# A gated MLP on one core: the opening of the first set reordered, one plain block fewer, and the second half of each block finished one step earlier

## The chip, the cores and the metric

The kernel runs on one core of a Trainium2 chip. The metric is device time in microseconds (us) of one execution, as the median over several runs. The core has five engines that run side by side and wait for one another through semaphores: TensorE (PE, matmuls into PSUM; PEld is its weight load), VectorE (DVE), ScalarE (ACT), GpSimd (POOL) and SyncE (SP, which issues DMAs). 16 DMA engines move data.

## The reference

x is 16 x 256 x 512 in f32 (4096 rows of 512), w1 is 512 x 4096, w2 is 2048 x 512.

```
h = x @ w1
gate, value = np.split(h, 2, axis=-1)
h = np.maximum(gate, 0) * value
return (h @ w2).astype(np.float32)
```

## The kernel before, in words

`fast_way` is the path that runs; `general_way` is a second one, taken only if sums of squares of the inputs (the `look` instructions on ScalarE, L190) come out of bounds. Everything is multiplied in f16 and summed in f32.

The 4096 rows are four **sets** of 1024, each set two halves of 512. The 2048 hidden columns are 16 **blocks** of 128; a block has a gate column and a value column of w1. Per set there are two stages. Stage 1 forms g = relu(gate) * value for 16 blocks. Stage 2 (`mm2_stream`, L279) multiplies g by w2 and writes the output.

Stage 1 uses a Strassen-Winograd scheme: seven products P1 to P7 (class `Block`, L195) in place of eight, each two matmuls of 512 columns. They need four sums of the x quarters (S1 to S4, `SUMS`, L185) and four sums of w1 quarters (T1 to T4, `TURNS`, L153) for each block. The products add up in three PSUM tiles: X, Y and W. P1 goes into X and ScalarE copies X into Y (L209). P5 goes into W, ScalarE scales it out as p5 (L216). P2 ends X. P6 adds to Y, ScalarE scales that out as u2 (L223). P3 ends W; VectorE forms c12 from W and u2 (L229) and then the first half of g from X and c12 (L230; called gX here). P7 adds to Y, VectorE forms c22 from Y and p5 (L235). P4 adds to Y; then `finish` forms the second half of g from Y and c22 (L241; called gY here).

The order is written out by hand. `SLOT` (L13) gives each product a place in a period of seven; P7 stands at 9 and P4 at 13, so they run in the period of the next block. A steady period on TensorE is P1, P5, P7 of the block before, P2, P6, P3, P4 of the block before, and in terms of one block j: P6(j), P3(j), P4(j-1), P1(j+1), P5(j+1), P7(j), P2(j+1), P6(j+1), P3(j+1), P4(j). The main loop (L540) emits `finish` of block j-1 only after P7 of block j (L552 to L554), so VectorE's order in a period is c12(j), gX(j), c22(j), gY(j-1). Every engine runs its instructions in the order in which they are emitted.

Stage 2 uses the same scheme with g in the place of x. It needs sums of g quarters (S1 to S4, L275, by GpSimd and for the last part by VectorE) and sums of w2 quarters (V). The w2 sums are made by DMA: SP copies parts of w2 (L532), GpSimd issues adding DMAs (`add_w2`, L163). Stage 2 of a set runs mostly behind stage 1 of that set, and its last 28 matmuls among the first blocks of the next set.

**The opening.** The first set can't use the scheme at once, since the w1 sums are not there yet. So its first `NPLAIN` = 4 blocks are plain: eight matmuls of 512 columns for each half of the rows (class `Plain`, L244). x comes as two loads of 512 KB through SP, and w1 columns 0 and 1 as two loads of 512 KB, in turn x, gates, x, values (L405 to L407). TensorE turns x by transposes (`turn_pair`, L371; `turn_half`, L379, for the second half of the rows, which GpSimd's queue loads as f16), VectorE and ScalarE copy the turned x to SBUF (L377, L384), and cast the w1 columns (`cast_w`, L390). The other w1 columns come in chunks (`CHUNKS`, L127) as casting DMAs on GpSimd's queue (`fetch_w1`, L350). Eight warm-up matmuls (`idle`, L171) run while nothing is there, and two more (`NFILL`) between the first turned x and the first gates. VectorE forms the x sums (`x_sum`, L449) beside the plain blocks of the second half.

GpSimd's own work in the first set, in its order (L523 to L539): w1 sums of blocks 4 to 11 two by two, with w2 loads between, then T1 and T2 of blocks 12 to 15, two adding DMAs, T3 and T4 of blocks 12 to 15, a third adding DMA, the load of x for set 2, then sums of g (L550). The w1 sums of blocks 0 to 3 are made by VectorE after the first set (L591).

Of the kernel before, what the change touches and what calls it, by code (L numbers as in the profile page):

```python
# [19 lines left out]
NWARM = 8  # L20
NFILL = 2
NPLAIN = 4
HIGH, LOW = 512.0, 32.0
# [76 lines left out]
def fast_way(ctx, tc, x2, w1, w2, out2, flag):  # L100
# [25 lines left out]

    CHUNKS = ((0, 2), (2, 2), (4, 2), (6, 2), (8, 4), (12, 4))  # L127
    place = {jb + i: (c, i) for c, (jb, n) in enumerate(CHUNKS) for i in range(n)}
# [66 lines left out]
    class Block:  # L195
# [41 lines left out]
        def P4(self):  # L237
            self.mm("P4", self.Y, False)

        def finish(self):  # L240
            nc.vector.scalar_tensor_tensor(out=self.g[:, self.jb, TH:], in0=self.Y, scalar=0.0,  # L241
                                           in1=self.c22, op0=MAX, op1=MULT)

    class Plain:  # L244
        def __init__(self, g, jb):
            self.g, self.jb = g, jb

        def open_x(self):
            self.X = psx.tile([P, TH], F32, name="X", tag="X")

        def open_w(self):
            self.W = psw.tile([P, TH], F32, name="W", tag="W")

        def mm(self, side, a, q, n=1):
            ts = slice(q * 256, (q + n) * 256)
            ps = self.W if side else self.X
            for e in range(4):
                name = (("B11", "B21"), ("B12", "B22"))[side][e // 2]
                nc.tensor.matmul(ps[:, ts], W(name, self.jb)[:, e % 2], a[:, e, ts], start=e == 0, stop=e == 3,  # L259
                                 skip_group_check=True)  # L260

        def close(self, h):
            v = tmp.tile([P, 2, TH], F32, name="v", tag="tmp")[:, 0]
            nc.scalar.activation(v, self.W, COPY, scale=GS)
            nc.vector.scalar_tensor_tensor(out=self.g[:, self.jb, h * TH:(h + 1) * TH], in0=self.X, scalar=0.0,
                                           in1=v, op0=MAX, op1=MULT)

# [11 lines left out]
    def mm2_stream(s, go):  # L279
# [14 lines left out]
        def step(name, b):  # L294
# [12 lines left out]
            elif name == "P2":  # L307
                yield from mm("P2", b, d["X"], False)
                d["o1"] = tmp.tile([P, DO], F32, name="o", tag="o", bufs=4)
                nc.scalar.activation(d["o1"][:, :HALF], d["X"], COPY, scale=1 / GS)  # L310
            elif name == "P6":
                yield from mm("P6", b, d["Y"], False)
                nc.scalar.activation(d["pu"][:, 1], d["Y"], COPY, scale=-1 / GS)
            elif name == "P3":
                yield from mm("P3", b, d["W"], False)
                nc.vector.scalar_tensor_tensor(out=d["o1"][:, HALF:], in0=d["W"], scalar=1 / GS, in1=d["pu"][:, 1],  # L316
                                               op0=MULT, op1=ADD)
                nc.sync.dma_start(out=out_v[s, 0, b], in_=d["o1"])
            elif name == "P7":
                yield from mm("P7", b, d["Y"], False)  # L320
                nc.vector.scalar_tensor_tensor(out=d["o2"][:, HALF:], in0=d["Y"], scalar=-1 / GS, in1=d["pu"][:, 0],
                                               op0=MULT, op1=ADD)
                if last and b == NB - 1:
                    nc.sync.dma_start(out=out_v[s, 1, b, :, HALF:], in_=d["o2"][:, HALF:])
            else:
                yield from mm("P4", b, d["Y"], False)
                nc.scalar.activation(d["o2"][:, :HALF], d["Y"], COPY, scale=1 / GS)
                if last and b == NB - 1:
                    nc.scalar.dma_start(out=out_v[s, 1, b, :, :HALF], in_=d["o2"][:, :HALF])
                else:  # L330
                    nc.sync.dma_start(out=out_v[s, 1, b], in_=d["o2"])
# [36 lines left out]
    xh = go["S2"][:, :NB]  # L368
    wl = g[:, NJ - 4:].rearrange("p a t -> p (a t)").bitcast(F32).rearrange("p (e g j) -> p e g j", e=4, g=2)

    def turn_pair(o, b0):  # L371
        for b in (b0, b0 + 1):
            ps = psw.tile([P, 4, P], F32, name="W", tag="W")
            for e in range(4):
# [4 lines left out]
    def turn_half(o, b0, copy):  # L379
        ps = psx.tile([P, 4, 2, P], F16, name="X", tag="X")  # L380
        for b in range(2):
# [7 lines left out]

    def cast_w(g_):  # L390
        nc.scalar.copy(out=wr[0][:, :2, g_], in_=wl[:, :2, g_])
        nc.vector.tensor_copy(out=wr[0][:, 2:, g_], in_=wl[:, 2:, g_])  # L392

# [10 lines left out]

    for i in range(2):  # L405
        nc.sync.dma_start(out=xf[:, 2 * i:2 * i + 2], in_=x_v[0, :, 2 * i:2 * i + 2])  # L406
        nc.sync.dma_start(out=wl[:, :, i], in_=w1_v[:, :, i, :2 * P])  # L407
    for t in ident.values():
        make_identity(nc, t)
    nc.gpsimd.tensor_copy(out=gate, in_=xf[:, 0, :1])  # L410
    fetch_w1(1, 0)
    fetch_w1(1, 1)
    for b in (0, 2):
        nc.gpsimd.dma_start(out=xh[:, b:b + 2], in_=x_v[0, :, NB + b:NB + b + 2])
# [4 lines left out]
    xo = x_tiles()  # L419
    plain = [Plain(g, jb) for jb in range(NPLAIN)]  # L420
    idle(NWARM)
    cast_w(0)
    turn_pair(xo, 0)
    idle(NFILL)
    plain[0].open_x()
    plain[1].open_x()
    for p in plain[:2]:
        p.mm(0, xo["A1"], 0)
    cast_w(1)
    turn_pair(xo, 2)  # L430
    for p in plain[:2]:
        p.open_w()
        p.mm(1, xo["A1"], 0)
    for p in plain[:2]:
        p.mm(0, xo["A1"], 1)
        p.mm(1, xo["A1"], 1)
        p.close(0)
    for p in plain[2:]:
        p.open_x()
        p.open_w()  # L440
        p.mm(0, xo["A1"], 0, 2)
        p.mm(1, xo["A1"], 0, 2)
        p.close(0)
        if p is plain[2]:
            turn_half(xo, 0, nc.vector.tensor_copy)
    turn_half(xo, 2, nc.scalar.copy)
    sums = list(SUMS)

# [3 lines left out]

    for p in plain:
        p.open_x()
        p.open_w()
        if p is plain[0]:
            for q in range(2):
                p.mm(0, xo["A2"], q)
                p.mm(1, xo["A2"], q)
        else:  # L460
            p.mm(0, xo["A2"], 0, 2)
            p.mm(1, xo["A2"], 0, 2)
        x_sum(xo)
        if p is not plain[-1]:
            p.close(1)
        look_x(0, p.jb)

    def look_w1(i):
        c, o = place[i // 2 * 2]
        look(wr[c][:, :, i % 2, o * P:(o + 2) * P], NX + i, 1024)  # L470

# [22 lines left out]
    for s in range(NS):  # L494
        for i in range(4 * NB):
            if s or i >= NPLAIN:
                LOOKS[s, i] = [lambda s=s, i=i: look_x(s, i)]
    LOOKS[0, NPLAIN].insert(0, lambda: plain[-1].close(1))

# [14 lines left out]
    for s in range(NS):  # L514
# [3 lines left out]
        blocks = {jb: Block(xo, g, jb) for jb in range(first, NJ)}  # L518
        plan = {jb * PERIOD + at: (jb, n) for jb in blocks for n, at in SLOT.items()}
        last = NJ * PERIOD  # L520
        stream = mm2_stream(s, go)
        if s == 0:
            w1_ops(nc.gpsimd, 4, 2)  # L523
            fetch_w2(0)
# [5 lines left out]
            w1_ops(nc.gpsimd, 10, 2)  # L530
            for to, v in ((V["T1"], V["B11"]), (v_12, w2_h[1]), (V["T4"], V["B21"])):
                nc.sync.dma_start(out=to, in_=v)  # L532
            for t in TURNS:
# [6 lines left out]
        for at in range(first * PERIOD, last + PERIOD):  # L540
            if at in plan:
                jb, n = plan[at]
                if n == "P1" and s and jb in (4, 8):
                    fetch_rows(s, 1 + jb // 4)
                if n == "P2" and s == 0 and jb in (11, 13, 15):
                    h = jb - 11
                    if h == 4:
                        add_w2("T4", "T2")
                    for m in ("S1", "S3")[:2 - h // 4]:
                        g_sum(nc.gpsimd, go, m, h, h + 2)  # L550
                getattr(blocks[jb], n)()
                ended = jb - (n == "P7") if n == "P7" or (n, jb) == ("P4", NJ - 1) else -1  # L552
                if ended in blocks:
                    blocks[ended].finish()  # L554
                if n == "P5":
                    for f in LOOKS.get((s, jb), ()):
                        f()
                if ended >= 0 and s:
                    if ended < NHC:
                        g_sum(nc.gpsimd, go, "S3", ended, ended + 1)  # L560
                        if s == 1 and ended in (1, 4):
                            cast_x(2 + ended // 4)
                    elif ended < NJ - BY_DVE:
                        for m in ("S1", "S2", "S4"):
                            g_sum(nc.gpsimd, go, m, ended - NHC, ended - NHC + 1)
            elif at >= last:
# [13 lines left out]
        if s + 1 < NS:  # L580
# [9 lines left out]
            if s == 0:  # L590
                w1_ops(nc.vector, 0, 2)  # L591
                w1_ops(nc.vector, 2, 2)
            advance(stream, MM2 - TAIL - 100 - done)
# [32 lines left out]
```

## Time and profile before

| | us |
|---|---|
| median of 3 runs | 312.03 (311.81 to 312.80) |
| the profiled execution | 312.03 |
| its span | 310.20 |
| TensorE busy | 301.7 |
| VectorE busy | 216.4 |
| ScalarE busy | 189.0 |
| GpSimd busy | 148.3 |
| granted TensorE clock | 1.00 |

The profile is one execution. Times in it run from the start of the span. A line of the order of time has the start, the duration, the engine, the line of the code (L followed by a number), the operation, the tiles that it writes and reads with their shapes, how many instructions are merged (x2), and in brackets the idle time of that engine just before and what ended it. SPq, POOLq and ACTq are DMA issues of an engine. Matmuls are pipelined: two of 512 columns are listed as 0.59 us, but the next two start 0.43 us after them.

### The profile page before, as it was taken

How to read it: one execution, taken by the hardware profiler on the slowest of the kernel's cores; microseconds unless marked ns; L12 is line 12 of the kernel's file. 1: busy time of each engine (PE TensorE's matmuls, PEld its weight loads, DVE VectorE, ACT ScalarE, POOL GpSimd, SP SyncE). 2: the span in 40 equal slices, each digit the busy share in tenths (PEclk: the TensorE clock that was granted, in tenths of full speed). 3: DMA queues.
4: the chain of work that ended last, by engine and by line, in shares of the span. 5: the costliest groups of instructions: out<-in, count | busy, mean ns of one | idle time of the engine just before them, and what ended most of it. 6: DMA issues, size and time to landing. Idle time of an engine off the chain costs nothing.

```text
span 310.2 us, 5097 instructions
## 1 busy us (share of the span) xinstructions
PE 301.7 (97%) x1867; PEld 183.0 (59%) x1867; DVE 216.4 (70%) x330; ACT 189.0 (61%) x450; POOL 148.3 (48%) x135
## 2 busy tenths in 40 slices
PE   8899999999999999999999999999999999999993
PEld 4654444588854444478874444458884444448883
DVE  1376888898548888884338888886526888888311
ACT  3347767647677667648847667656857667673230
POOL 5779997950003537992001435995000433898000
PEclk9999999999999999999999999999999999999999
DMA  7999979998315370045220110028311100000113
GB/s 246 200 202 204 215 195 231 203 120 231 121 73 101 71 169 0 3 92 158 90 104 35 34 34 2 0 52 151 139 71 68 34 6 30 0 2 0 69 68 139
DMA packets 33449, 30.74 MB, mean 99 GB/s; under 512 B 13872, under 2 KB 27952, under 8 KB 33200
## 3 DMA queue, kind: packets, MB, share of 16 engines
q0 software_dynamic: 10704, 11.54, 23.1%
q1 hardware_dynamic: 22576, 18.75, 20.5%
q8 instruction: 15, 0.25, 0.4%
q10 hardware_dynamic: 144, 0.13, 0.1%
q14 instruction: 10, 0.08, 0.1%
HBM read 24.12 MB, written 11.53 MB: 115 GB/s over the span
## 4 chain that ended last, share of the span: by engine, by line
PE 92%; DMA 2%; DVE 2%; issue 1%; ACT 1%; SPq 0%; DVEq 0%
PE Y L202 25%; PE X L202 17%; PE W L202 17%; PE Y L286 13%; PE W L286 8%; PE X L286 8%; DMA g<-in_w_dram 2%; PE W L259 2%; PE X L259 2%; DVE g_S L275 1%; ACT x_A L384 0%; SPq L406 0%; DVE wr L392 0%; DVE g L241 0%; DVE x_A L377 0%
## 5 line engine op out<-in xcount | busy, mean ns | idle before, releaser
L275 POOL TENSOR_TENSOR g_S<-g 128x512 f16<-128x512 f16 (+1 forms) x47 | 60.5, 1330 | 125.3 <-DVE g L241 123.4
L202 PEld LDWEIGHTS <-wt 128*128 128x128 f16 x480 | 46.9, 98 | 55.0 <-issue 0.2
L202 PE MATMUL X<-x_A,wr 128*128 128x512 f16 x240 | 71.4, 379 | 0.2 <-ACT Y L209 0.2
L202 PE MATMUL Y<-x_S,wt 128*128 128x512 f16 x240 | 71.4, 379 | 0.0
L202 PEld LDWEIGHTS <-wr 128*128 128x128 f16 x360 | 35.2, 98 | 41.1 <-issue 0.5
L229 DVE SCALAR_TENSOR_TENSOR cc<-W,pu 128x512 f32<-128x512 f32 x60 | 41.5, 692 | 23.8 <-ACT pu L223 23.7
L209 ACT COPY Y<-X 128x512 f32<-128x512 f32 x60 | 34.2, 570 | 37.7 <-PE X L202 37.1
L286 PEld LDWEIGHTS <-g_S 128*128 128x128 f16 x512 | 49.9, 98 | 6.4 <-DVE g_S L275 0.6
L235 DVE SCALAR_TENSOR_TENSOR cc<-Y,pu 128x512 f32<-128x512 f32 x60 | 41.5, 691 | 6.2 <-PE Y L202 0.2
L223 ACT ACTIVATE pu<-Y 128x512 f32<-128x512 f32 x60 | 35.8, 597 | 14.3 <-PE Y L202 14.3
L230 DVE SCALAR_TENSOR_TENSOR g<-X,cc 128x512 f16<-128x512 f32 x60 | 41.5, 691 | 2.3
L286 PEld LDWEIGHTS <-g 128*128 128x128 f16 x384 | 37.6, 98 | 8.2
L241 DVE SCALAR_TENSOR_TENSOR g<-Y,cc 128x512 f16<-128x512 f32 x60 | 40.8, 681 | 1.8 <-PE Y L202 1.8
L216 ACT ACTIVATE pu<-W 128x512 f32<-128x512 f32 x60 | 36.1, 602 | 0.0
L202 PE MATMUL W<-x_S,wr 128*128 128x512 f16 x120 | 35.7, 379 | 0.0
L202 PE MATMUL W<-x_S,wt 128*128 128x512 f16 x120 | 35.7, 379 | 0.0
L202 PE MATMUL Y<-x_A,wt 128*128 128x512 f16 x120 | 35.7, 379 | 0.0
L286 PE MATMUL X<-w,g 128*128 128x256 f16 x256 | 31.2, 272 | 0.0
L286 PE MATMUL Y<-v,g_S 128*128 128x256 f16 x256 | 30.6, 273 | 0.0
L316 DVE SCALAR_TENSOR_TENSOR o<-W,pv 128x256 f32<-128x256 f32 x16 | 6.8, 423 | 30.4 <-PE W L286 30.4
L275 POOL TENSOR_TENSOR g_S<-g,g_S 128x512 f16<-128x512 f16 x18 | 21.8, 1210 | 1.4
L275 POOL TENSOR_TENSOR g_S<-g_S,g 128x512 f16<-128x512 f16 x18 | 21.3, 1186 | 1.4
(69 smaller groups left out, 297.4 us busy)
## 6 DMA issues: line engine op xcount, KB each, us to landing
out_dram<-o SPq DMA_DIRECT2D x16, 256.0 KB, 2.2
out_dram<-pv SPq DMA_DIRECT2D x15, 256.0 KB, 2.0
x<-in_x_dram POOLq DMA_DIRECT2D x3, 1024.0 KB, 8.0
xn<-x SPq DMA_DIRECT2D x12, 256.0 KB, 3.2
wr<-in_w_dram POOLq DMA_DIRECT2D x4, 512.0 KB, 14.5
w<-in_w_dram POOLq DMA_DIRECT2D x4, 512.0 KB, 11.8
wr<-in_w_dram POOLq DMA_DIRECT2D x6, 256.0 KB, 8.8
g_S<-in_x_dram SPq DMA_DIRECT2D x2, 512.0 KB, 4.7
```

The lines of the kernel that those rows point to most:

```text
L202: nc.tensor.matmul(ps, W(wn, self.jb)[:, b], self.xo[xn][:, b, :], start=fresh and b == 0, stop=b == 1, skip_group_check=True)
L209: nc.scalar.copy(out=self.Y, in_=self.X)
L216: nc.scalar.activation(self.p5, self.W, COPY, scale=GS)
L223: nc.scalar.activation(self.u2, self.Y, COPY, scale=-GS)
L229: nc.vector.scalar_tensor_tensor(out=self.c12, in0=self.W, scalar=GS, in1=self.u2, op0=MULT, op1=ADD)
L230: nc.vector.scalar_tensor_tensor(out=self.g[:, self.jb, :TH], in0=self.X, scalar=0.0, in1=self.c12, op0=MAX, op1=MULT)
L235: nc.vector.scalar_tensor_tensor(out=self.c22, in0=self.Y, scalar=-GS, in1=self.p5, op0=MULT, op1=ADD)
L241: nc.vector.scalar_tensor_tensor(out=self.g[:, self.jb, TH:], in0=self.Y, scalar=0.0, in1=self.c22, op0=MAX, op1=MULT)
L259: nc.tensor.matmul(ps[:, ts], W(name, self.jb)[:, e % 2], a[:, e, ts], start=e == 0, stop=e == 3, skip_group_check=True)
L275: eng.tensor_tensor(go[n][:, h0:h1], go[i0][:, h0:h1], go[i1][:, h0:h1], op=op)
L286: nc.tensor.matmul(ps, go[gn][:, k, b * P:(b + 1) * P], V[vn][:, k, :], start=fresh and k == 0, stop=k == NHC - 1, skip_group_check=True)
L316: nc.vector.scalar_tensor_tensor(out=d["o1"][:, HALF:], in0=d["W"], scalar=1 / GS, in1=d["pu"][:, 1], op0=MULT, op1=ADD)
```

## The change

1. **Finishing.** `finish` is gone; its instruction (L241 before) is now the end of `P4`. So it is emitted ahead of c22 of the next block. Work of GpSimd that followed it (sums of g) is emitted after P4 too. In the first set the GpSimd sums S1 and S3 are emitted at P1 instead of P2.
2. **Opening.** Both x loads come first. Then come the gates of column 0, the gates of column 1, the values of both, and column 2 in two loads, all as f32 through SP and cast on ScalarE and VectorE. GpSimd's queue loads the second x half in two pieces, the second one only after the gates of column 1 have landed. Chunk 2 of w1 (casting DMA) now has columns 3 to 5.
3. **Plain blocks.** Three in place of four. The second half of the rows is worked in steps of a quarter set (256 columns), all three blocks of the first quarter, then all of the second. One warm-up matmul fewer between. Block 3 becomes a full `Block` (`lead`); its P1 stands between the gates and the values of the last plain step.
4. **Weight sums.** GpSimd makes the sums of block 3 ahead of those of blocks 4 and 5. VectorE makes those of blocks 0 to 2 later.
5. **w2.** The copies into v_12 are two of 512 KB instead of one of 1024 KB; copies are now T1, T3, T2, T4.
6. **Output.** In the last set the first half's output tile leaves in two DMAs.

```diff
-NFILL = 2
-NPLAIN = 4
+NFILL = 1
+NPLAIN = 3
...
-    CHUNKS = ((0, 2), (2, 2), (4, 2), (6, 2), (8, 4), (12, 4))
+    CHUNKS = ((0, 2), (2, 1), (3, 3), (6, 2), (8, 4), (12, 4))
...
         def P4(self):
             self.mm("P4", self.Y, False)
-
-        def finish(self):
             nc.vector.scalar_tensor_tensor(out=self.g[:, self.jb, TH:], in0=self.Y, scalar=0.0,
                                            in1=self.c22, op0=MAX, op1=MULT)
...
-                nc.sync.dma_start(out=out_v[s, 0, b], in_=d["o1"])
+                for n in (slice(0, HALF), slice(HALF, DO)) if last else (slice(0, DO),):
+                    nc.sync.dma_start(out=out_v[s, 0, b, :, n], in_=d["o1"][:, n])
...
-    for i in range(2):
-        nc.sync.dma_start(out=xf[:, 2 * i:2 * i + 2], in_=x_v[0, :, 2 * i:2 * i + 2])
-        nc.sync.dma_start(out=wl[:, :, i], in_=w1_v[:, :, i, :2 * P])
+    for b in (0, 2):
+        nc.sync.dma_start(out=xf[:, b:b + 2], in_=x_v[0, :, b:b + 2])
+    fetch_wl(0, 0)
+    fetch_wl(1, 0)
+    fetch_wl(0, 1, 2)
+    fetch_wl(2, 0)
+    fetch_wl(2, 1)
...
-    nc.gpsimd.tensor_copy(out=gate, in_=xf[:, 0, :1])
-    fetch_w1(1, 0)
-    fetch_w1(1, 1)
-    for b in (0, 2):
+    for b, land in ((0, xf[:, 0, :1]), (2, wl[0][:, 0, 0, P:P + 1])):
+        nc.gpsimd.tensor_copy(out=gate, in_=land)
         nc.gpsimd.dma_start(out=xh[:, b:b + 2], in_=x_v[0, :, NB + b:NB + b + 2])
...
+    whole = [Plain(g, jb, xo["A1"], 0, 0, 2) for jb in range(NPLAIN)]
+    parts = [[Plain(g, jb, xo["A2"], 1, q, 1) for jb in range(NPLAIN)] for q in range(2)]
+    lead = Block(xo, g, NPLAIN)
...
+    idle(NWARM)
+    turn_pair(xo, 0, psw, "W")
+    cast_w(0, 0)
+    idle(NFILL)
+    turn_pair(xo, 2, psx, "X")
+    whole[0].gates((0,))
+    cast_w(1, 0)
+    whole[0].gates((1,))
+    whole[1].gates()
+    cast_w(0, 1)
+    cast_w(1, 1)
+    whole[0].values()
+    whole[0].close()
+    cast_w(2, 0)
+    whole[1].values()
+    turn_half(xo, 0, nc.vector.tensor_copy)
+    whole[1].close()
+    cast_w(2, 1)
+    part(whole[2])
+    part(parts[0][0])
+    part(parts[0][1])
+    turn_half(xo, 2, nc.scalar.copy)
+    part(parts[0][2])
+    x_sum(xo)
+    for p in parts[1][:2]:
+        part(p)
+        x_sum(xo)
+        look_x(0, p.jb)
+    parts[1][2].gates()
+    lead.P1()
+    parts[1][2].values()
+    look_x(0, 2)
+    x_sum(xo)
...
         if s == 0:
+            w1_ops(nc.gpsimd, 3, 1)
             w1_ops(nc.gpsimd, 4, 2)
...
-            for to, v in ((V["T1"], V["B11"]), (v_12, w2_h[1]), (V["T4"], V["B21"])):
-                nc.sync.dma_start(out=to, in_=v)
+            for m, v in (("T1", "B11"), ("T3", "B12"), ("T2", "B22"), ("T4", "B21")):
+                nc.sync.dma_start(out=V[m], in_=V[v])
...
-                if n == "P2" and s == 0 and jb in (11, 13, 15):
+                if n == "P1" and s == 0 and jb in (11, 13, 15):
...
                 getattr(blocks[jb], n)()
-                ended = jb - (n == "P7") if n == "P7" or (n, jb) == ("P4", NJ - 1) else -1
-                if ended in blocks:
-                    blocks[ended].finish()
...
-                if ended >= 0 and s:
+                if n == "P4" and s:
...
-                w1_ops(nc.vector, 2, 2)
+                w1_ops(nc.vector, 2, 1)
```

## The prediction

> **What bounds the kernel now.** I read the page's busy table and its chain, then the order of time on the engines at the opening, inside one steady block, and at the end of the first set.
>
> ```profile
> PE 301.7 (97%) x1867; PEld 183.0 (59%) x1867; DVE 216.4 (70%) x330; ACT 189.0 (61%) x450; POOL 148.3 (48%) x135
> ...
> PE 92%; DMA 2%; DVE 2%; issue 1%; ACT 1%; SPq 0%; DVEq 0%
> ```
>
> TensorE is the bound. A change gains only where TensorE stands or where matmuls go; it loses wherever another engine comes late once in each block. TensorE's waits lie in the opening and at one place at 71 us:
>
> ```profile
> 10.68 1.03 PE L259 MATMUL W<-x_A,wr 128*128 128x256 f16 x8 [1.51 <-DVE x_A L377]
> ...
> 26.25 0.59 PE L202 MATMUL X<-x_A,wr 128*128 128x512 f16 x2 [0.23 <-ACT Y L209]
> ```
>
> After 31 us it stands once, 0.34 us at 71.37 for VectorE's S4. Now a steady block, TensorE, then ScalarE, then VectorE:
>
> ```profile
> 57.38 0.59 PE L202 MATMUL Y<-x_A,wt 128*128 128x512 f16 x2
> ...
> 59.53 0.59 PE L202 MATMUL Y<-x_S,wt 128*128 128x512 f16 x2
> ...
> 60.40 0.59 PE L202 MATMUL Y<-x_A,wt 128*128 128x512 f16 x2
> ```
> ```profile
> 57.15 0.60 ACT L223 ACTIVATE pu<-Y 128x512 f32<-128x512 f32 x1 [0.25 <-PE Y L202]
> ```
> ```profile
> 57.77 0.69 DVE L229 SCALAR_TENSOR_TENSOR cc<-W,pu 128x512 f32<-128x512 f32 x1 [0.20 <-ACT pu L223]
> 58.50 0.69 DVE L230 SCALAR_TENSOR_TENSOR g<-X,cc 128x512 f16<-128x512 f32 x1
> 59.30 0.69 DVE L235 SCALAR_TENSOR_TENSOR cc<-Y,pu 128x512 f32<-128x512 f32 x1
> 59.91 0.68 DVE L241 SCALAR_TENSOR_TENSOR g<-Y,cc 128x512 f16<-128x512 f32 x1
> ```
>
> P4 of the block before starts at 57.38, this block's at 60.40: 3.02 us for 14 matmuls, 0.216 each. VectorE's L235 (c22) reads Y after P7, and P4 adds into that same Y, so P4 may not start before c22 has ended. It ends at 59.99, 0.41 before P4. L241 finishes the block before, and no matmul waits for it at once. Last, GpSimd from 45 us, and VectorE behind it:
>
> ```profile
> 45.06 0.94 POOL L163 DMA_DIRECT2D v_T<-w  x1
> 48.36 0.88 POOL L163 DMA_DIRECT2D v<-w  x1 [2.36 <-DMA v<-w]
> 48.95 2.44 POOL L160 TENSOR_TENSOR wt<-wr 128x1024 f16<-128x1024 f16 x1
> 51.03 2.43 POOL L160 TENSOR_TENSOR wt<-wr,wt 128x1024 f16<-128x1024 f16 x1
> 53.10 1.19 POOL L163 DMA_DIRECT2D v<-v_T  x1
> 53.68 1.15 POOL L359 DMA_DIRECT2D x<-in_x_dram  x1
> 54.24 8.98 POOL L275 TENSOR_TENSOR g_S<-g 128x1024 f16<-128x1024 f16 x4
> 62.57 1.49 POOL L163 DMA_DIRECT2D v_T<-v  x1
> 63.20 3.02 POOL L275 TENSOR_TENSOR g_S<-g 128x1024 f16<-128x1024 f16 x1
> ```
> ```profile
> 64.80 1.97 DVE L275 TENSOR_TENSOR g_S<-g 128x1024 f16<-128x1024 f16 x1
> 66.70 2.35 DVE L275 TENSOR_TENSOR g_S<-g_S,g 128x2048 f16<-128x2048 f16 x2
> 68.97 2.35 DVE L275 TENSOR_TENSOR g_S<-g,g_S 128x2048 f16<-128x2048 f16 x2
> ```
>
> GpSimd works without a pause from 48.36 to 66.22. VectorE's second S2 (at 66.70 + half of 2.35 = 67.8) needs GpSimd's last S1, done at 66.22: 1.6 us to spare. From that S2 on, two S4 follow, and the second one's end at 71.32 releases TensorE at 71.37.
>
> **Part 1, the finishing step ahead of c22 (all blocks).** No instruction is added; L241 and L235 change places on VectorE. TensorE's order is P6, P3, P4 of the block before, P1, P5, P7, and so on, so the new VectorE order is c12, gX, gY of the block before, c22. From the rows: c12 starts 57.77; gX follows 0.73 later; gY, whose P4 ran at 57.38, needs nothing more and follows at the back-to-back step of 59.91 - 59.30 = 0.61; c22 another 0.61 later; it takes 0.68. End: 57.77 + 0.73 + 0.61 + 0.61 + 0.68 = 60.40. TensorE follows VectorE by 0.05 (71.32 to 71.37). P4 can start at 60.45 instead of 60.40. The cover of 0.41 is gone and 0.05 is late. This does not stay 0.05: a late P4 delays P1, P5, P7, P2 and P6 behind it on TensorE, that P6 releases ScalarE's L223, which releases the c12 of the block two later, and so its P4. So about 0.05 is added every second block. In a set of 16 blocks that is 8 times 0.052 (0.052 being the same sum with the unrounded starts), 0.41 us; in sets 2 to 4 **1.25 us**, since no gap in TensorE's order of time there gives anything back. Bounds: VectorE's step could be 0.1 shorter, then nothing; or c22 0.05 later still, then 2.5 us. I take 1.25, as each term is a measured step.
>
> **Part 2, the opening.** Two of 64 plain matmuls go (48 plain and 14 of block 3): 2 x 0.216 = 0.43. One warm-up matmul goes (0.74 for two): 0.36. Block 3's P1 has the last plain values between it and P5, so the 0.23 at 26.25 goes. Sum 1.0. The waits for loads change: four 512 KB loads are used at about 4.3, 6.0, 7.8 and 9.22, so 1.63 us for 512 KB. Now both x halves come first (4.3, 5.95), then two single columns at 0.82 to 1.63 each: 0.82 if bytes cost, 1.63 if pieces cost (a single column has as many pieces as a pair). x has 2 KB pieces and w 1 KB, and both take the same time for their bytes, so I take 0.9. That puts the value columns at 9.4, with their cast at 10.3 to 10.9 when the second x half shares the engines. Gates of columns 0 and 1 keep TensorE busy to about 9.8. I expect 0.5 to 1.1 waiting there, up to 0.7 for the cast of column 2 (behind a finish and the turned x on VectorE's queue), 0.4 for ScalarE's 1.01 copy of the second x half: 0.9 to 2.2, against 1.51 + 0.30 + 0.27 before. So TensorE reaches block 4 **1.2 us** earlier (-0.5 to 2.2).
>
> **Part 3, GpSimd.** Column 3 becomes a full block, so GpSimd gets its four weight sums: a quarter of 1024 wide. 512 wide steps by 1.11, or 1.60 beside VectorE's x sums; half of that gives 0.6 to 0.85 each, **2.6 us** together. They stand ahead of everything GpSimd does in this set. They start when chunk 2's weights land: before, 4 loads x 1.63 + 6 cast loads x 1.37 (GpSimd's issue waits step 10.91, 12.43, 13.71, 15.03) = 14.7, landing for the start at 17.53. Now 3 x 1.63 + 4 x 0.9 + 5 x 1.37 = 15.3: start 18.1 (17.8 to 21.1). GpSimd is 3.2 late (2.7 to 7).
> It regains some. The doubled copy into v_12 is cut in two, so the 2.36 wait at 48.36 goes. The first add is issued at 48.3, the second at 48.9, the block 12 sums run 49.4 to 53.6. But the third add (T2 += T1) needs the first landed; such adds take 5.8 to 6.7 in the DMA table, so 54.7 with 6.4: GpSimd waits 1.1 there, and is 1.6 late (0.5 to 4) against 53.10. The last S1 ends 67.8, and 0.2 later for lying beside more of VectorE's S1 and S2. VectorE's second S2 then starts at 68.0 instead of 67.8, and TensorE passes 71.37 **0.2 us late**. The 1.2 of the opening is gone: it was taken from TensorE, and GpSimd ends the first set.
> On a rule: VectorE's 1.97 at 64.80 beside GpSimd's 3.02, where a quarter of 8.98 (2.24) is usual, shows them slowing each other. The Trainium skill (SBUF — State Buffer, Who interferes with whom) says that a VectorE instruction with two SBUF inputs contends with a GpSimd one that reads SBUF, and that the loser blocks for the whole instruction. By it, as an estimate, S1 would end one whole S2 step of 1.2 later rather than 0.2, and the time would be 314.5 instead of 313.5.
>
> **Part 4, at no cost.** Last set's o1 leaves in two halves: four more SP issues of 0.3 to 0.4 each, behind which SP idles, while ScalarE's issue at 305.94 ends the run; uncovered, at most 0.4. VectorE's sums for column 3 (4 x 0.35 at 78 us) go, GpSimd's S1 and S3 are issued a product earlier but in the same order, SP gets one more copy at 34 us with nothing behind it until the turned x at 63.85: 0, up to 0.1.
>
> **Sum.** The profiled execution took 312.03 (span 310.20, the rest around it), equal to the median. 312.03 + 0.2 + 1.25 = **313.5**.
>
> **Rivals.** (a) VectorE's loop fits after all (gY follows gX a little sooner) while GpSimd still takes the opening: 312.03 + 0.2 = 312.2. For it: 0.05 is small. Against it: every step is a row. (b) The loop costs, but GpSimd is only 0.5 late, and 0.9 of the opening stays: 312.4. (c) Both go well, faster than before: 312.03 - 0.9 = 311.1, and 310.8 at best with all 1.2 kept; its point of decision is c22 ending 0.05 sooner and the sums of column 3 starting by 17.8. (d) Single columns cost by pieces: GpSimd starts near 20, S1 ends 1.3 to 2.4 later, 314.8 to 315.9. The change doing nothing of what it says I don't count: matmuls do go.
>
> **Chances.** Forecast 0.46, (a) 0.15, (b) 0.13, (c) 0.12, (d) 0.14. About 0.3% (0.94 us) is what a measurement of this kernel can tell from no change. Slower: forecast and (d), 0.60. Same: (a) and (b), 0.28. Faster: (c), 0.12. The range 311.0 to 315.0 leaves out half of (c) and half of (d).
>
> **What would show it.** P4's matmuls with a small wait for VectorE's c22 in every second block, and blocks 3.05 instead of 3.02 apart in sets 2 to 4. The first sum on GpSimd near 18.1, no 2.36 wait, instead one of about 1.1 ahead of the third add. TensorE at block 4 about 1.2 earlier, and a wait near 67 for S1. If blocks stay 3.02 apart, part 1 is wrong; if the third add starts by 53.1, part 3 is.

## The result and the profile after

| | before | after |
|---|---|---|
| median, us | 311.92 (311.75 to 312.80, 4 runs) | 315.68 (314.62 to 316.70, 4 runs) |
| profiled execution, its span | 312.03, 310.2 | 315.71, 313.9 |
| ratio after/before | | 1.0114, 95% interval 1.0076 to 1.0153 |

Slower, as forecast (313.5), but by 3.7 us where 1.5 was forecast, and above the range. First the busy table of the page and its chain (share of the span by engine, then by line):

```profile
PE 303.6 (97%) x1868; PEld 182.1 (58%) x1868; DVE 210.8 (67%) x339; ACT 190.7 (61%) x458; POOL 149.4 (48%) x138
...
PE 78%; POOL 11%; DMA 5%; issue 3%; DVE 1%; SPq 0%; ACT 0%; POOLq 0%; DVEq 0%
PE Y L202 21%; PE X L202 14%; PE W L202 14%; PE Y L286 13%; POOL wt L160 8%; PE W L286 8%; PE X L286 8%; DMA wr<-in_w_dram 2%; DMA g<-in_w_dram 2%; DVE g_S L275 1%; POOL w L357 1%; POOL v L163 0%; SPq L413 0%; POOL wr L353 0%; POOL g_S L423 0%
```

GpSimd works 1.1 us more in all, yet it went from no share of the chain to 11%, and 8% is L160: its sums of w1 quarters. TensorE is no longer alone at the bound in the first set. To see where the time came in, take one fixed matmul of each set (number 100 of its stage 2, counted from 0) from both traces:

| start of that matmul, us | set 1 | set 2 | set 3 | set 4 | end of span |
|---|---|---|---|---|---|
| before | 73.13 | 145.95 | 218.77 | 291.79 | 310.25 |
| after | 75.76 | 148.84 | 221.92 | 295.20 | 313.93 |
| added on the way | 2.63 | 0.26 | 0.26 | 0.26 | 0.27 |

So 2.63 came in the first set, 0.78 in the three others, 0.27 at the very end. The matmul of set 1 is called the marker from here on. TensorE in order of time (start, duration, engine, line, operation, idle time before it and what ended it), first the one wait near the end of the first set before:

```profile
71.37 1.48 PE L286 MATMUL W<-w,g_S 128*128 128x256 f16 x12 [0.34 <-DVE g_S L275]
```

After:

```profile
9.08 1.96 PE L250 MATMUL X<-x_A,wr 128*128 128x256 f16 x12 [1.01 <-ACT wr L395]
11.31 1.90 PE L250 MATMUL W<-x_A,wr 128*128 128x512 f16 x8 [0.27 <-ACT wr L395]
...
24.09 0.59 PE L202 MATMUL X<-x_A,wr 128*128 128x512 f16 x2
25.04 0.60 PE L202 MATMUL W<-x_S,wt 128*128 128x512 f16 x2 [0.36 <-POOL wt L160]
...
30.70 0.59 PE L202 MATMUL X<-x_A,wr 128*128 128x512 f16 x2
31.43 0.60 PE L202 MATMUL W<-x_S,wt 128*128 128x512 f16 x2
...
54.06 0.60 PE L202 MATMUL Y<-x_S,wt 128*128 128x512 f16 x2 [0.46 <-POOL wt L160]
...
56.14 0.60 PE L202 MATMUL Y<-x_A,wt 128*128 128x512 f16 x2 [0.18 <-POOL wt L160]
...
70.60 0.61 PE L286 MATMUL Y<-v,g_S 128*128 128x256 f16 x4
71.73 1.48 PE L286 MATMUL Y<-v,g_S 128*128 128x256 f16 x12 [0.52 <-DVE g_S L275]
...
74.00 1.48 PE L286 MATMUL W<-w,g_S 128*128 128x256 f16 x12 [0.35 <-DVE g_S L275]
```

The bracket understates a standstill, as ends of matmuls are modelled; starts are exact. Two matmuls of 512 columns need 0.43 from start to start, so 24.09 to 25.04 is 0.52 too long, and 30.70 to 31.43 is 0.30 too long though no bracket stands there. Counted so, TensorE waits for GpSimd's weight sums by 0.52, 0.30, 0.29 (at 37.82), 0.62 and 0.34: 2.07. Add 0.20 for five late P4 (at 30.27, 36.66, 43.05, 49.13 and 62.24), and 0.69 at 71.73, a wait that the kernel before doesn't have; the one at 74.00 is 0.51 in both (at 71.37 before). Before had 0.39 at 26.25 and 0.05. The sum is 2.5, nearly all of the first set's 2.63. In this profile the opening gained next to nothing: P1 of block 4 starts at 24.09 and not 25.00, but P7 and P4 of block 3 (four matmuls, 0.86) come after it now.

GpSimd after:

```profile
9.57 0.23 POOL L422 COPY gate<-g 128x1 f32<-128x1 f32 x1 [4.25 <-DMA g<-in_w_dram]
10.04 0.73 POOL L423 DMA_DIRECT2D g_S<-in_x_dram  x1 [0.24 <-issue]
...
19.45 0.67 POOL L160 TENSOR_TENSOR wt<-wr 128x256 f16<-128x256 f16 x1 [2.73 <-DMA wr<-in_w_dram]
20.20 0.99 POOL L160 TENSOR_TENSOR wt<-wr,wt 128x256 f16<-128x256 f16 x1
21.15 1.20 POOL L160 TENSOR_TENSOR wt<-wr 128x256 f16<-128x256 f16 x1
22.31 1.12 POOL L160 TENSOR_TENSOR wt<-wr,wt 128x256 f16<-128x256 f16 x1
...
50.02 0.94 POOL L163 DMA_DIRECT2D v_T<-w  x1
50.65 1.21 POOL L163 DMA_DIRECT2D v<-w  x1
...
55.40 1.51 POOL L163 DMA_DIRECT2D v<-v_T  x1
...
65.47 3.37 POOL L275 TENSOR_TENSOR g_S<-g 128x1024 f16<-128x1024 f16 x1
```

The first sum starts at 19.45 (17.53 before), block 3's four take 3.94 to 23.39. The first add is issued at 50.02, 4.96 late; the 2.36 wait of the second is gone; the last S1 ends at 68.84, 2.63 late by the unrounded times. VectorE beside it:

```profile
66.64 2.77 DVE L275 TENSOR_TENSOR g_S<-g 128x1024 f16<-128x1024 f16 x1
69.33 2.35 DVE L275 TENSOR_TENSOR g_S<-g_S,g 128x2048 f16<-128x2048 f16 x2
```

VectorE's S1 ends at 69.41, and before it ended at 66.77: both times 0.56 after GpSimd's S1 (66.22 before) by the unrounded times. Its S2 and S4 follow without a gap. So the marker moved by the same 2.63 as GpSimd's last S1. Last, the loop in set 2, TensorE and VectorE:

```profile
133.14 0.59 PE L202 MATMUL W<-x_S,wr 128*128 128x512 f16 x2
133.60 0.59 PE L202 MATMUL Y<-x_A,wt 128*128 128x512 f16 x2
134.03 0.59 PE L202 MATMUL X<-x_A,wr 128*128 128x512 f16 x2
```
```profile
132.27 0.68 DVE L239 SCALAR_TENSOR_TENSOR g<-Y,cc 128x512 f16<-128x512 f32 x1
132.86 0.68 DVE L235 SCALAR_TENSOR_TENSOR cc<-Y,pu 128x512 f32<-128x512 f32 x1
```

c22 (L235) is behind gY (L239) and ends at 133.54; P4 starts at 133.60, 0.46 behind P3 where 0.43 is enough. The P4 of the blocks before and after it are late by 0.015.

### The profile page after: what moved, and what is told of

Its sections match the earlier page's. It is cut to its first block, busy times and chain, and to the rows that moved or that the text cites. A ratio compares the mean times of both kernels' runs of the same rounds, so it can differ in the third digit from the quotient of the medians.

```text
span 313.9 us, 5176 instructions
## 1 busy us (share of the span) xinstructions
PE 303.6 (97%) x1868; PEld 182.1 (58%) x1868; DVE 210.8 (67%) x339; ACT 190.7 (61%) x458; POOL 149.4 (48%) x138
## 4 chain that ended last, share of the span: by engine, by line
PE 78%; POOL 11%; DMA 5%; issue 3%; DVE 1%; SPq 0%; ACT 0%; POOLq 0%; DVEq 0%
PE Y L202 21%; PE X L202 14%; PE W L202 14%; PE Y L286 13%; POOL wt L160 8%; PE W L286 8%; PE X L286 8%; DMA wr<-in_w_dram 2%; DMA g<-in_w_dram 2%; DVE g_S L275 1%; POOL w L357 1%; POOL v L163 0%; SPq L413 0%; POOL wr L353 0%; POOL g_S L423 0%
## 5 line engine op out<-in xcount | busy, mean ns | idle before, releaser
L202 PE MATMUL Y<-x_S,wt 128*128 128x512 f16 x244 | 72.6, 379 | 0.5 <-POOL wt L160 0.5
L202 PE MATMUL X<-x_A,wr 128*128 128x512 f16 x244 | 72.5, 378 | 0.0
L230 DVE SCALAR_TENSOR_TENSOR g<-X,cc 128x512 f16<-128x512 f32 x61 | 42.2, 691 | 2.4
L239 DVE SCALAR_TENSOR_TENSOR g<-Y,cc 128x512 f16<-128x512 f32 x61 | 41.5, 680 | 2.8 <-PE Y L202 2.8
L235 DVE SCALAR_TENSOR_TENSOR cc<-Y,pu 128x512 f32<-128x512 f32 x61 | 41.5, 681 | 0.2
L216 ACT ACTIVATE pu<-W 128x512 f32<-128x512 f32 x61 | 36.8, 603 | 0.8 <-DVE g L230 0.4
```

What stands on the lines that cost most here:

```text
L202: nc.tensor.matmul(ps, W(wn, self.jb)[:, b], self.xo[xn][:, b, :], start=fresh and b == 0, stop=b == 1, skip_group_check=True)
L216: nc.scalar.activation(self.p5, self.W, COPY, scale=GS)
L230: nc.vector.scalar_tensor_tensor(out=self.g[:, self.jb, :TH], in0=self.X, scalar=0.0, in1=self.c12, op0=MAX, op1=MULT)
L235: nc.vector.scalar_tensor_tensor(out=self.c22, in0=self.Y, scalar=-GS, in1=self.p5, op0=MULT, op1=ADD)
```

## The experiments

Ratios are to the kernel before, run on the same chip. The marker (before 73.13, after 75.76) is from the one profiled execution, which can lie well off the median: e2's is the slowest of its runs, those of e3, e7, e10 and e14 are the fastest.

**1. The finishing step, alone and undone.** e1 is the kernel before with gY at the end of `P4`:

```diff
-        def finish(self):
             nc.vector.scalar_tensor_tensor(out=self.g[:, self.jb, TH:], in0=self.Y, scalar=0.0,
```

> The kernel before, with the finishing step moved to P4 (ahead of c22) and nothing else. In the changed kernel's trace every second P4 of a steady block waits for VectorE, 0.043 us for each pair of blocks. Theory (the loop through c22 costs on its own, about 0.34 us a set): 311.92 + 4 x 0.3 = 313.1, and P4 gaps of about 0.03 and 0.015 in turn. Rival (all of the loss is in the opening): 311.9 to 312.2.

Measured: 313.25, ratio 1.0031 (1.0017 to 1.0045). Its sets 2 to 4 are 0.28 longer each, close to the 0.26 of the changed kernel: the late P4 is real. Its marker is 73.63, 0.50 later than before, and there the finishing step isn't shown to be the cause: the copy that GpSimd waits for at 48.36 let it go on at 48.86, and GpSimd's last S1, VectorE's S1 and the marker all came 0.50 later. e2 is the changed kernel with `finish` behind c22 again:

> The changed kernel with the finishing step put back behind c22 (and the first set's g sums at P2, as before). Theory (sets 2 to 4 lose 1.05 through the loop, the first set is ruled by GpSimd and gains nothing): 315.7 - 1.05 = 314.6, with blocks 3.02 apart and TensorE still past the S4 wait near 74.0. Rival (the loop is also what makes GpSimd late at the end of the first set): 313.5 or less.

Measured: 313.37, ratio 1.0036 (1.0022 to 1.0050). Sets 2 to 4 take what they took in the kernel before (72.82, 72.82 and 73.02). The median fell by 2.3, more than the 0.8 of the loop, to where the rival put it; where the other 1.5 come from is open. Its profile doesn't show the rival's reason, and it is the clearest test of part 3. The opening is unchanged, but here the first gates land early (cast at 6.87, in the profile after at 8.62), and GpSimd's first sum starts at 18.05, as predicted. The predicted wait ahead of the third add is there as well:

```profile
6.87 0.41 ACT L397 CAST wr<-g 128x256 f16<-128x256 f32 x1
```
```profile
18.05 0.67 POOL L160 TENSOR_TENSOR wt<-wr 128x256 f16<-128x256 f16 x1 [2.98 <-DMA wr<-in_w_dram]
...
55.34 0.86 POOL L163 DMA_DIRECT2D v<-v_T  x1 [0.72 <-DMA v_T<-w]
...
65.52 2.61 POOL L277 TENSOR_TENSOR g_S<-g 128x1024 f16<-128x1024 f16 x1
```
```profile
65.14 3.55 DVE L277 TENSOR_TENSOR g_S<-g 128x1024 f16<-128x1024 f16 x1
```

TensorE is at block 4 1.66 earlier than before (P1 at 22.48, and four matmuls more to come), and yet the marker is at 75.05, 1.92 later than before: the gain, and more, is lost to GpSimd, whose last S1 ends 1.91 later.

**2. Is it the second gate?** e3 is the changed kernel with both pieces of the second x half issued without the wait for the gates of column 1:

```diff
-        nc.gpsimd.tensor_copy(out=gate, in_=land)
+        if b == 0:
+            nc.gpsimd.tensor_copy(out=gate, in_=land)
```

> The changed kernel without the second gate on GpSimd's queue, so that the second x half and chunk 2 of w1 are asked for right behind the first piece, from about 5.3 us instead of 10.0. Theory (the gate opened at 9.57 and made chunk 2 land late, at 19.3): GpSimd's first sum starts near 18 and all that it ends in the first set is 1.2 to 1.5 earlier: 314.3. Rival (the DMA engines were full anyway, so chunk 2 lands at the same time, and the early w columns land later in addition): 315.7 to 316.5.

Measured: 314.02, ratio 1.0076 (1.0055 to 1.0098), marker 73.58. The first sum starts at 17.33 instead of 19.45, the waits for weight sums at 25, 31 and 38 are gone, GpSimd's last S1 ends at 66.66 and VectorE's S1 at 67.22, 0.56 later. Without the wait for the gate the kernel is 1.2 (by the ratios) to 1.7 us (by the medians) faster. How much of the 2.1 at the first sum is the gate is less clear: in this profile the first column of w1 lands at 6.71, in the one after at 8.60, and in e2, which has the gate and lands at 6.85, the first sum starts at 18.05.

**3. Is it block 3's sums?** e4 gives them to VectorE, two behind each x sum; e8 leaves them out in set 1 (block 3's first 1024 rows are then computed from other operands).

```diff
+        for t in TURNS[2 * p.jb:2 * p.jb + 2]:
+            w1_one(nc.vector, NPLAIN, 1, *t)
...
-            w1_ops(nc.gpsimd, 3, 1)
```

> The changed kernel with the four weight sums of block 3 formed by VectorE (two behind x sum S2, two behind S4) instead of ahead of all else on GpSimd, where they took 3.94 us. Theory (GpSimd's chain of the first set sets its end): GpSimd starts the sums of blocks 4 and 5 at 19.4, S1 ends about 3.9 earlier, TensorE passes the S4 wait near 71 instead of 74: 312.8. Rival (the landing of the weights and not GpSimd's work sets it): 315 or more, as the start at 19.4 stays.

Measured: 316.17, ratio 1.0123 (1.0098 to 1.0148), not what I expected. Its first gates land as late as in the profile after (cast at 8.69). GpSimd's last S1 ends at 66.33 and TensorE's waits at 71.73 and 74.00 are gone, but others took their place:

```profile
24.11 0.60 PE L202 MATMUL W<-x_S,wt 128*128 128x512 f16 x2 [1.36 <-DVE wt L160]
...
27.04 0.59 PE L202 MATMUL W<-x_S,wr 128*128 128x512 f16 x2 [1.16 <-DVE x_S L436]
...
28.91 0.60 PE L202 MATMUL Y<-x_S,wt 128*128 128x512 f16 x2 [0.42 <-DVE x_S L436]
```
```profile
24.09 1.12 DVE L160 TENSOR_TENSOR wt<-wr,wt 128x256 f16<-128x256 f16 x1
25.14 0.41 DVE L265 SCALAR_TENSOR_TENSOR g<-X,v 128x256 f16<-128x256 f32 x1
25.47 1.42 DVE L436 TENSOR_TENSOR x_S<-x_A,x_S 128x1024 f16<-128x1024 f16 x1
26.82 0.28 DVE L160 TENSOR_TENSOR wt<-wr 128x256 f16<-128x256 f16 x1
```

The same sum of 256 took VectorE 1.12 beside GpSimd's and 0.28 when it found a gap. Marker 76.88.

> The changed kernel with the four weight sums of block 3 left out of the first set: its products P4 to P7 there use raw quarters of w1 instead, so block 3 of the first 1024 rows is not what the reference has; VectorE makes these sums after the first set. No other engine gets more work in the opening. Theory (GpSimd's chain sets the first set): everything on GpSimd is 3.5 to 3.9 earlier, its last S1 ends near 65, TensorE passes the S4 wait near 71.5, where its own matmuls hold it: 313.3. Rival (the late landing of the weights sets it, whatever GpSimd does): 315 or more.

Measured: 312.76, ratio 1.0041 (1.0015 to 1.0068), marker 72.16; GpSimd's last S1 ends at 64.82, and TensorE has no wait for it. By the profiles the first set without these four sums is 3.6 shorter than after and 1.0 shorter than before, but this execution is 0.43 below its median. By the medians the run is 0.84 above the kernel before, and the loop's 0.78 is still in it: without the four sums the first set loses next to nothing. Some of the 3.6 is the first sum's start, 17.75 here.

**4. Is it GpSimd's last S1, through VectorE?** e5 (changed kernel) and e6 (kernel before) let VectorE do that S1 in one instruction with its own:

```diff
-                    for m in ("S1", "S3")[:2 - h // 4]:
+                    for m in ("S1", "S3") if h < 4 else ():
...
-            g_sum(nc.vector, go, "S1", 6, 8)
+            g_sum(nc.vector, go, "S1", 4, 8)
```

> The changed kernel with GpSimd's last S1 of the first set (blocks 4 and 5) given to VectorE, which now forms S1 of blocks 4 to 7 in one instruction. So far VectorE's last S1 ended 0.55 to 0.57 us after GpSimd's last S1 in every trace (66.77 after 66.22 before, 69.41 after 68.84 changed, 67.22 after 66.66 without the second gate): the two do not run beside each other, and GpSimd's end sets S2, S4 and TensorE. Theory: without it VectorE starts at 66.6, the sums take 1.13 each, TensorE passes the S4 wait near 72.3 instead of 74.0, and the time is 314.0. Rival (S4 waits for something else, as the 1.6 us to spare of the prediction would have it): 315.7.

> The same edit in the kernel before. Theory: GpSimd's end at 66.22 set S4 there too, so TensorE's wait at 71.37 goes (0.5 us with its step): 311.7. Rival (1.6 us to spare, as the prediction said, VectorE was only slow): the longer S1 on VectorE costs what it saves, 312.2.

Measured: e5 313.34, ratio 1.0059 (1.0036 to 1.0081); e6 311.60, ratio 0.9990 (0.9981 to 0.9999), the only version ahead of both kernels, by 0.3 us, which is at the edge of what these runs can tell apart. e6's VectorE:

```profile
64.90 1.23 DVE L275 TENSOR_TENSOR g_S<-g 128x2048 f16<-128x2048 f16 x1
66.05 2.35 DVE L275 TENSOR_TENSOR g_S<-g_S,g 128x2048 f16<-128x2048 f16 x2
```

Twice the columns in 1.23, where half of them beside GpSimd took 1.97: splitting this sum between the two engines gained nothing. TensorE's wait at 71.37 is gone. e5 gained more than expected, and its runs lie 312.1 to 316.0 apart, so one profile of it says little; it still shows TensorE waiting for weight sums at 35.7, 52.0 and 54.1 (0.28, 0.62 and 0.34).

**5. GpSimd later, with the opening of before.** e10 is the kernel before with block 4's four sums made twice; e13 is the same on e6.

```diff
+            w1_ops(nc.gpsimd, 4, 1)
             w1_ops(nc.gpsimd, 4, 2)
```

> The kernel before, with GpSimd making the four weight sums of block 4 twice (the same values again): about 2.6 to 4 us more at the head of its chain in set 1, and nothing else changed. Theory (VectorE's S1 ends 0.55 after GpSimd's last S1 in every trace, so TensorE at 71.37 follows GpSimd by what is left once the wait of 2.36 at 48.36 is used up): GpSimd's last S1 ends 0.3 to 1.5 later than 66.22, TensorE's wait for VectorE's S4 grows from 0.34 by the same, and the time is 312.2 to 313.4. The step as predicted (1.6 us to spare ahead of VectorE's second S2): nothing at TensorE, 311.9 to 312.0. Rival: the whole delay passes on, 314.5 or more.

> As e10 (the kernel before, block 4's sums twice), with GpSimd's last S1 given to VectorE as in e6. Theory (what GpSimd is late with reaches TensorE through its last S1, ahead of VectorE's S1, S2 and S4): the 1.15 of e10 goes, 311.6 to 312.0, runs within 1.4 us. Rival (it reaches TensorE through the w1 sums of blocks 4 to 15, which P5 waits for): 312.8 to 313.3, as wide as e10.

Measured: e10 313.14 (312.16 to 314.91), ratio 1.0041 (1.0023 to 1.0059); e13 312.33 (311.32 to 314.97), ratio 1.0012 (0.9991 to 1.0033). The profiled execution of e10 is one of its two fastest. There the wait at 48.36 takes up nearly all of the delay:

```profile
47.20 0.94 POOL L163 DMA_DIRECT2D v_T<-w  x1
48.52 0.88 POOL L163 DMA_DIRECT2D v<-w  x1 [0.39 <-issue]
...
63.35 3.02 POOL L275 TENSOR_TENSOR g_S<-g 128x1024 f16<-128x1024 f16 x1
```
```profile
64.78 2.15 DVE L275 TENSOR_TENSOR g_S<-g 128x1024 f16<-128x1024 f16 x1
66.85 2.35 DVE L275 TENSOR_TENSOR g_S<-g_S,g 128x2048 f16<-128x2048 f16 x2
```

GpSimd's last S1 ends 0.16 later than before, VectorE's S1 0.16 later (66.93), and the marker 0.16 later (73.29): nothing to spare. The same holds in every profile in which GpSimd makes this S1, VectorE's S1 overlaps it and TensorE then waits. In us later than before:

| | GpSimd's last S1 ends | VectorE's S1 ends | marker |
|---|---|---|---|
| e10 | 0.16 | 0.16 | 0.16 |
| e3 | 0.45 | 0.45 | 0.45 |
| e1 | 0.50 | 0.50 | 0.50 |
| e2 | 1.91 | 1.92 | 1.92 |
| after | 2.63 | 2.64 | 2.63 |

The other runs of e10 are up to 2.75 us slower than this one, with the opening unchanged: with the 2.36 nearly used up, the runs spread. e13 took back 0.8 of 1.15, so the last S1 is one way of a late GpSimd to TensorE. Its runs spread as widely, and its profile has a wait of 0.34 for a weight sum at 55.04, so it isn't the only one.

**6. Which loads of the opening?** e7 mends four things in the changed kernel (e2, e3, e5 together, and o1 in one DMA). e9 is e7 with the gates of columns 0 and 1 in one load of 1 KB pieces. e11 is e7 with column 2 by GpSimd's queue together with column 3, as before the change. e12 is e11 with the two SP loads of column 2 issued, for nothing. e14 is the changed kernel with only e11's edit, the core of which is:

```diff
-    CHUNKS = ((0, 2), (2, 1), (3, 3), (6, 2), (8, 4), (12, 4))
+    CHUNKS = ((0, 2), (2, 2), (4, 2), (6, 2), (8, 4), (12, 4))
...
-    fetch_wl(2, 0)
-    fetch_wl(2, 1)
...
         nc.gpsimd.dma_start(out=xh[:, b:b + 2], in_=x_v[0, :, NB + b:NB + b + 2])
+        if b == 0:
+            fetch_w1(1, 0)
+            fetch_w1(1, 1)
```

> The changed kernel without the second gate, with the finishing step behind c22, with the whole output tile in one DMA, and with GpSimd's last S1 given to VectorE. Theory: each cause found is taken away, the opening's gain of about 0.4 to 0.9 and the 0.5 at S4 stay: 311.0 to 311.5, faster than the kernel before (312.2). Rival (something in the opening itself, plain steps or single columns, costs): 312.2 or more.

> As e7 (changed kernel with no second gate, the finishing step behind c22, o1 in one DMA, the last S1 on VectorE), but the gates of columns 0 and 1 come as one load of 512 KB in pieces of 1 KB in place of two single columns of 256 KB in pieces of 512 B. What is open after e7 is why runs of the new opening lie 311.5 to 314.6 where runs of the opening before lie within 1.4 us. Theory A (single columns, by their small pieces, are what one DMA engine or SP's issue comes late with): the median falls to 311.5 (311.2 to 312.0) and the runs lie within 1.4 us. Rival B (not these two loads: the order of the opening, or the seven loads deep queue on SP): the median stays near 312.7 and the runs lie 2 us or more apart.

> As e7, but column 2 of w1 isn't loaded alone as f32 by SP in two loads: it comes with column 3 as a casting load on GpSimd's queue as before the change, issued behind the first piece of the second x half. SP has five opening loads in place of seven, and ScalarE and VectorE four casts less. Theory A (the depth of SP's queue is what makes the runs scatter): 311.2 (310.9 to 311.6), runs within 1.4 us. Rival B (the single columns of the gates, which stay here, are what scatters): runs 2 us or more apart, median 312.3 or more. Rival C (column 2 now lands too late for its plain block): TensorE waits ahead of the third plain block, 312.5 to 314 with little scatter.

> As e11 (column 2 by GpSimd's queue), with the two loads of column 2 by SP put back as idle loads: they are issued and land, and nothing reads them. SP's queue is seven deep again, GpSimd's chain is as in e11. Theory A (seven opening loads on SP make one DMA engine or SP's issue late, and that is what scatters): runs 2 us or more apart again, median 312.6 or more, and one DMA engine behind the others in the profile. Theory B (what scatters is that GpSimd's first sum waits for a landing and its chain has no slack; in e11 the first sum follows the last issue without a wait): runs as in e11, median 312.2 (311.9 to 312.5).

> The changed kernel with column 2 by GpSimd's queue as in e11, and nothing else mended: second gate, the finishing step early, o1 in two DMAs and GpSimd's last S1 stay. By the parts measured so far: loop 0.8 and tail 0.27 stay, GpSimd's first sum starts 2 to 4 us earlier than at 19.45, so the first set loses 0 to 0.8 in place of 2.6: 313.4 (313.0 to 314.0). Rival (the seven loads on SP are not where the first set loses): 315 or more.

| | median (lowest to highest) | ratio, interval | marker |
|---|---|---|---|
| e7 | 312.75 (311.48 to 314.55) | 1.0036, 1.0018 to 1.0053 | 72.55 |
| e9 | 312.67 (311.67 to 313.84) | 1.0014, 0.9998 to 1.0031 | 73.75 |
| e11 | 312.16 (311.07 to 313.76) | 1.0007, 0.9992 to 1.0021 | 72.42 |
| e12 | 313.16 (313.08 to 313.58) | 1.0037, 1.0023 to 1.0050 | 73.87 |
| e14 | 313.12 (312.33 to 313.95) | 1.0037, 1.0023 to 1.0052 | 72.72 |

e7 missed: its best run is where I put it, its median 1.3 above. e9: the runs still spread by 2.2, so the small pieces are not the reason for that; by the ratios e9 is 0.2% below e7, but the intervals overlap. e14 is the telling one: with columns 2 and 3 loaded as before, 2.5 of the 3.7 us are gone. It changes two things at once: SP has two loads fewer, and the load with column 3, which GpSimd's first sum needs, is issued ahead of the second gate. Its GpSimd and VectorE:

```profile
7.69 0.18 POOL L420 COPY gate<-g 128x1 f32<-128x1 f32 x1 [0.80 <-DMA g<-in_w_dram]
...
15.67 0.68 POOL L160 TENSOR_TENSOR wt<-wr 128x256 f16<-128x256 f16 x1
...
61.82 2.72 POOL L275 TENSOR_TENSOR g_S<-g 128x1024 f16<-128x1024 f16 x1
```
```profile
64.91 0.69 DVE L275 TENSOR_TENSOR g_S<-g 128x1024 f16<-128x1024 f16 x1
65.52 2.35 DVE L275 TENSOR_TENSOR g_S<-g_S,g 128x2048 f16<-128x2048 f16 x2
```

The first sum follows the last issue, waiting for no landing, 3.8 us earlier than after and 2.4 earlier than in e2; GpSimd's S1 is done at 64.54, before VectorE's S1 starts, which then takes 0.69 and not 2.77. TensorE waits for no sum of g. With the other causes mended, columns 2 and 3 loaded as before are worth less: e11 is 0.3% below e7 by the ratios. e12 fits neither theory: no spread, but 1.0 slower than e11. Its two idle loads go ahead of the casting loads on the DMA engines, and the third plain block waits 1.32, where e11 has a wait of 0.36:

```profile
13.52 1.04 PE L252 MATMUL X<-x_A,wr 128*128 128x512 f16 x4 [1.32 <-DMA wr<-in_w_dram]
```

The order on the DMA engines is my reading; the run itself shows only that two more loads on SP cost 1.0 (512 KB took 1.63 in the opening of before), and that in its six runs they bring no spread.

## Why the prediction was wrong, step by step

- **Part 1, the loop: right in kind, mis-sized.** P4 waits for c22 behind gY, as worked out. Predicted 0.41 a set and 1.25 in all; measured 0.26 and 0.78. The term that was too large is the 0.052 for two blocks, eight times: P4 is late by 0.03 and 0.015 in turn, 0.043 for two blocks, and in set 2 that holds for 14 of its 16 blocks, not for the first and the last (seven times 0.043 is 0.30, close to the 0.26). e1 and e2 show the same size, put on and taken off.
- **Part 2, the opening: the gain came, but not in the profile after.** Predicted 1.2 earlier at block 4 (its own terms give 0.9 to 2.2, with 1.5 in the middle). On equal matmuls it is 0.05 after, but 1.66 in e2, 1.88 in e5 and 0.99 in e8, whose loads are the same. What is different after is one late landing: of the 16 shares of the first single column (one for each DMA engine) 15 had landed by 6.57 and the last came at 8.60, so ScalarE's cast of the first gates waited until 8.62 and the second gate opened at 9.57. In e4 it is 8.66; in the six other profiles with seven loads on SP (e2, e3, e5, e7, e8, e12) the last share comes at 6.62 to 6.97. Whether the changed kernel's other runs have it is not known.
- **Part 3, GpSimd: the step that failed.** It said that GpSimd is 1.6 late at the third add, that VectorE's second S2 leaves "1.6 us to spare", and so that TensorE passes 71.37 "0.2 us late". Three things stand in its place. First, GpSimd is 2.3 late at the third add: the first sum comes at 19.45 instead of 18.1 (within its bounds), as the second gate opens at 9.57 behind the late landing, and the four sums take 3.94 instead of 2.6. I had halved 512-wide rows, 0.85 at most; the three that lie beside VectorE took 0.99 to 1.20. The wait of 1.1 at the third add didn't come: so late, the first add has landed. In e2, where the start and this wait came as predicted, the third add is still 2.2 late. Second, and this is the step itself, there is nothing to spare. I put the need at the second S2 by its operands; but VectorE's S1, which shares no operand with GpSimd's, ends 0.56 after GpSimd's S1 in all seven profiles in which they overlap (before, after, e1, e2, e3, e8, e10), and takes 0.69 in e4 and e14 where they don't. So what GpSimd's last S1 is late reaches TensorE in full: 1.92 for 1.91 in e2, 2.63 for 2.63 after. Third, GpSimd reaches TensorE not only at the end: 2.07 us are waits for weight sums at five places, none of which the prediction looked at. These waits take up part of the 2.63 on the way; without the S1 on GpSimd (e5) three of them stay. Block 4's sums were done in time before; with 3.94 ahead of them they are not.
- **The rule that I weighed and left.** The Trainium skill (SBUF — State Buffer, Who interferes with whom) has the loser of VectorE and GpSimd blocked for the whole instruction. The row of 1.97 beside GpSimd's 3.02, which I read as two engines slowing each other, fits such a block of VectorE: 1.03 (e8) to 3.55 (e2) beside GpSimd, 0.69 alone, and always the same 0.56 after GpSimd's end. GpSimd wasn't slowed: its last S1 took 0.30 more than the sum before it in e14 too (2.72 and 2.42), where VectorE's S1 hadn't begun. In e2 VectorE's S1 starts 0.38 ahead of GpSimd's by the profile and is the one that waits all the same. The estimate by the rule, 314.5, was nearer than mine, and still only had the S1 late by itself.
- **Part 4: not quite free.** From the last matmul to the end it is 5.30 instead of 5.04. In profiles with o1 in two DMAs it is 4.87 to 5.77, with o1 whole 4.89 to 5.59, so the two DMAs aren't shown to be the cause. Part of it lies behind the last landing: from there to the end of the span it is 1.71 in all five profiles of the kernel before and its variants, 2.21 after, and 1.84 to 2.22 in the other ten. Why stays open.
- **Rivals.** (d), single columns by pieces with GpSimd starting near 20, came nearest in time, but not in cause: in e2, e5 and e8 the same single columns land in time and GpSimd starts at 17.5 to 18.1, and the 19.45 after is the late landing. The two loads of column 2 on SP cost 1.0 in e12, with the rest mended.
- **What stays open.** Why the runs spread by 2 to 4 us once GpSimd's chain has no slack. e10 shows that the opening isn't needed for it, and e12 that seven loads alone don't bring it. Two landings differ between profiles of the same loads: the first single column (6.62 to 8.66), and the copy that GpSimd's second add waits for in the kernel before (the add starts at 48.36, in e1 at 48.86, in e13 at 49.88). That they make the spread is a guess, as there is one profile of each kernel, and what makes them late is not shown.

## What to carry to other kernels

Before you add work to the head of an engine's chain, list every consumer along that chain, not only the last one: a wait of 2.36 us near its end hides a delay only for what comes after it. Slack between two engines that share a path is not read from operands: look at whether the one's end follows the other's end in the profile. A moved load is judged by what it pushes back: with columns 2 and 3 loaded as before, 2.5 of the 3.7 us were gone. And before a late landing is put down to the change, look for it in other profiles of the same loads: here six of eight didn't have it.

## What the runs showed of the hardware

VectorE's sum of 128x1024 in f16 took 0.69 alone and 1.03, 1.97, 2.15, 2.37, 2.77 and 3.55 beside GpSimd's, always ending some 0.56 after it. In the profile of the changed kernel one of the 16 DMA engines brought its share of the first single column at 8.60, when the 15 others had brought theirs by 6.57; in e14 the last came 0.07 after the rest. SP needed 3.80 for its five issues of w1 (4.01 in e12) and 1.57 for three (e14): four of the five took about 0.5 each after, and one took 1.53.
